# A hybrid attention and GLA layer: work beside the projections held to its place, key, GLA and merge transposes later, key tiles in other buffers

## The chip, the cores and the metric

One core of a Trainium2 chip. The metric is device time of one execution in microseconds (us); the kernel before took 2056.09 us, the median of three runs (2054.43 to 2057.13).

## The reference, cut to what matters

One layer over 256 latent tokens with 256 context tokens ahead, width 2048, all in float32. Two token mixers work side by side on one input projection.

```python
h  = rms_norm(x, g_mix) * (1 + scale) + shift         # shift, scale, gates: silu(c) @ w_mod + b_mod
qa, ka, va, qb, kb, vb, rb, lrf, lrb, gate_a, gate_b = split(h @ w_in)
o_attn = windowed_attention(rope(rms_norm(qa)), rope(rms_norm(ka)), va, ctx keys and values, sink)
o_gla  = latent_gla(qb, kb, vb, gf, gb, end states of the context)      # 4 heads, both directions
y = sigmoid(gate_a) * (o_attn @ w_attn_o) + sigmoid(gate_b) * ((rms_norm(o_gla) * silu(rb)) @ w_gla_o)
x = x + gate * (y @ w_out)
x = x + gate2 * conv_ffn(modulate(rms_norm(x)))
```

## The kernel before, in words

**Projections.** Every projection multiplies by weights streamed from memory in pieces of 256 x 512 float32 (512 KB). `wsplit` (L156) loads a piece (`raw`, 7 buffers), ScalarE copies it to `whi` (L61), and VectorE subtracts to `wlo` (L62), 3 buffers each. For each left side a product is then three matmuls: high and low part of the left side by `whi`, high part by `wlo`. `proj_nat` (L165) leaves tokens on the partitions, one bank of 512 columns for each left side (four with the context: 24 products a piece; two without: 12 products, and 8 pieces a block of columns); `proj_T` (L185) leaves features there. Four accumulation banks are shared by all; `evac` copies a finished bank.

**Order of the stages.** Five groups of the first projections while the modulation is computed; a low-rank gate; four GLA heads, each beside one projection (`with_gla`, L639, with the generator `gla_A`, L491); the keys of the attention (KA, `ka_evac`, L705) and its values (VA); queries and attention; the GLA's output gate (RB, `rb_evac`, L821); four rounds of merge, each of GA, `w_attn_o`, GB, `w_gla_o` (`mg_evac`, L855); `w_out`; the feed-forward part.

**Work beside.** Ahead of each piece `tick` (L133) is called. It takes the deferred functions from the front of the list `later` whose count has run out (transposes mostly, put there by `defer`), advances the generator in `beside` by its rate, and takes steps from `bg_steps` at `bg_rate`. These steps (`mod_latent`, L242) compute the later modulation: they load a 512 KB piece of `w_mod` into the same 7 `raw` buffers and multiply and add it on VectorE (`macc`, L266); after eight pieces a column sum is taken and a small product `pcl` (L276) deferred. The rate is 0.3 in the GLA heads, 1.6 in KA and VA, 0.52 from RB on.

**What sets the order.** A scheduler orders each engine's instructions; `wsplit` has a raised priority. Nothing but data ties a small product issued in a tick to the large products around it. All loads keep their order on SyncE's queue.

**The places of the change.** In a GLA head, `gla_A` yields after each of eight levels (products `pa`, L534) and, after the tiles kf and kg are made by scans, exponentials and two multiplications (L579 to L593), once before their products (L599), which `gla_o` (L605) needs. `norm_rope` (L682) takes a bank to a normalised, rotated tile: copy y (tag fc), squares sq (tag fc), sum, reciprocal root, products; the tile ends in sq. The tag fc has 6 buffers, fa 4; fa holds the GLA's and the attention's tiles. `to_T` (L813) transposes a finished tile for RB and the merge (`pto`), `turn` in `ka_evac` the key tiles (`ptk`).

Of the kernel before, what the change touches and what calls it, by code (L numbers as in the profile page):

```python
# [16 lines left out]
P = 128  # L17
# [13 lines left out]
def layer_kernel(ctx, tc, A, out):  # L31
# [28 lines left out]
    def split(hi, lo, src):  # L60
        S.activation(hi, src, AF.Copy)  # L61
        V.tensor_tensor(lo, src, hi.bitcast(F32), op=ALU.subtract)  # L62

# [69 lines left out]
    def tick():  # L133

        for e in later:
            e[0] -= 1
        while later and later[0][0] < 0:
            later.pop(0)[1]()
# [6 lines left out]
        while bg_rate[1] >= 1.0 and bg_steps:  # L145
            bg_rate[1] -= 1.0
            bg_steps.pop(0)()

# [16 lines left out]
    def proj_nat(w, r0, c0, kts, lhs, evac):  # L165

        banks = [acc.tile([P, 512], F32, name="acc", tag="acc") for _ in lhs]
        for k0 in kts[::2]:
# [3 lines left out]
            for i, l in enumerate(lhs):  # L172
                for k in range(nk):
                    kt = k0 + k
                    ahi, alo = l(kt)
                    PE.matmul(banks[i], ahi, hi[:, k, :], start=(kt == kts[0]), stop=False)  # L176
                    PE.matmul(banks[i], alo, hi[:, k, :], start=False, stop=False)  # L177
            for i, l in enumerate(lhs):
                for k in range(nk):
                    kt = k0 + k  # L180
                    PE.matmul(banks[i], l(kt)[0], lo[:, k, :], start=False, stop=(kt == kts[-1]))  # L181
# [3 lines left out]
    def proj_T(w, c0, kts, rhs, evac):  # L185
# [4 lines left out]
        for k0 in kts[::2]:  # L190
# [3 lines left out]
            for part in range(2):  # L194
                for f in range(4):
                    for k in range(nk):
                        kt = k0 + k
                        w_ = (lo if part else hi)[:, k, f * P:(f + 1) * P]
                        for i, r in enumerate(rhs):
# [3 lines left out]
                            PE.matmul(o, w_, ahi, start=(kt == kts[0] and b == 0 and part == 0),  # L203
                                      stop=(kt == kts[-1] and part == 1), skip_group_check=True)
                            if part == 0:
                                PE.matmul(o, w_, alo, start=False, stop=False, skip_group_check=True)  # L206
# [35 lines left out]
    def mod_latent(parts):  # L242
# [11 lines left out]
        def step(i):  # L254
# [13 lines left out]
            if k0 == KT - 2:  # L268
# [5 lines left out]
                def out():  # L274
                    pc = bank("pcl", (32, 16))
                    PE.matmul(pc, sel[:, 0:32], rs, start=True, stop=True)  # L276
# [11 lines left out]
    def rows_from_cols(name, col):  # L288

        pt = bank("pt_" + name, (KT, P), side=True)  # L290
        PE.transpose(pt, col, ident)
# [199 lines left out]
    def gla_A(h, kb, qb, res):  # L491
# [7 lines left out]
        for d in range(2):  # L499
            g_ = W2("fc", "gc", [P, 2, T])  # L500
            for dt in range(2):
                f = 2 * h + dt
                pz = bank("pz", side=True)
                PE.matmul(pz, wg[:, f * P:(f + 1) * P], lr[:, d, :], start=True, stop=True)
# [14 lines left out]
        for t in range(2):  # L519
            for dt in range(2):  # L520
                PE.matmul(pa[:, t, :], k_[:, dt, t * P:(t + 1) * P], q_[:, dt, t * P:(t + 1) * P],
# [7 lines left out]
        def products(lv, q2, k2):  # L529
            pa = bank("pa", (P, 2, P), side=True)  # L530
            for t in range(2):
                tq = t if lv < 7 else 1 - t
                for dt in range(2):
                    PE.matmul(pa[:, t, :], k2[:, dt, t * P:(t + 1) * P],  # L534
# [59 lines left out]
        yield  # L594
        pa = bank("pa", (P, 2, T), side=True)
        for t in range(2):
            for i, (kk, qq) in enumerate(((kf, q2), (kg, q3))):
                for dt in range(2):
                    PE.matmul(pa[:, t, :], kk[:, dt, t * P:(t + 1) * P], qq[:, dt, :],  # L599
# [5 lines left out]
    def gla_o(h, a, vh, vl):  # L605
# [3 lines left out]
        for t in range(2):  # L609
            po = bank("po", side=True)  # L610
            n = 0
            for s in range(4):
# [6 lines left out]
                for x_, y_ in ((ah, vh), (ah, vl), (al, vh)):  # L619
                    PE.matmul(po, x_, y_[:, s, :], start=(n == 0), stop=(n == 11))  # L620
# [18 lines left out]
    def with_gla(h, kb, block):  # L639
        res = []  # L640
        beside[:] = [gla_A(h, kb, qbt, res), 1.5, 0.0]
# [40 lines left out]
    def norm_rope(b, r, t):  # L682

        y = W2("fc", "y", [P, 4, P])
# [20 lines left out]
    def ka_evac(i, b):  # L705
        z = norm_rope(b, rk if i < 2 else None, i % 2)

        def turn():
            pt = bank("ptk", (P, 4, P))
            for h in range(4):  # L710
                PE.transpose(pt[:, h, :], z[:, h, :], ident)
            split(kTh[:, :, i * P:(i + 1) * P], kTl[:, :, i * P:(i + 1) * P], pt)

        defer(1 + i // 2, turn)
# [7 lines left out]
    def qa_block(g):  # L722
        qT = M("qT", [P, 2, 4, T], F32R)

        def evac(t, b):
            z = norm_rope(b, rq, t)
# [279 lines left out]
```

## Time and profile before

| | |
|---|---|
| median of three runs | 2056.09 us |
| profiled execution | 2061.47 us, span 2059.7 us, mean granted clock 0.989 |
| GLA heads | 232 to 485 us |
| KA and VA | 485 to 580 us |
| queries, attention, GA | 580 to 800 us |
| RB | 800 to 853 us |
| merge | 853 to 1205 us |
| w_out, feed-forward part | 1205 to 2060 us |

The lines in the next sections are from one profiled execution, in us. PE is TensorE, DVE VectorE, ACT ScalarE, SP SyncE, POOL GpSimd. A row of the timeline has start, length, engine, line and operation, what it writes and reads, a count of equal neighbours, and in brackets how long the engine waited ahead of it and for what. A row of the windows has the stretch, its length, the busy time of each engine with its instructions, the granted clock, the share of the DMA engines and their GB/s.

### The profile page before, as it was taken

Reading aid. Unit: us, or ns where it says so; the run is one execution under the profiler, and the core shown is the slowest. Engines: PE = TensorE matmul, PEld = TensorE weight load, DVE = VectorE, ACT = ScalarE, POOL = GpSimd, SP = SyncE. Lnnn points to the kernel's source line nnn. Section 1 sums busy time; section 2 is a strip of 40 time slices with the busy share of each in tenths; the row PEclk is TensorE's granted clock in tenths of the full one; section 3 lists DMA queues with packets and bytes.
Section 4 is the critical chain, followed back from the end, with each engine's and each line's share of the span. In section 5 each row is a group of like instructions: output and inputs, shape, how many; then the busy total and the mean of one; then the engine's idle time right before and its main releaser. Section 6 shows DMA issues by size and latency. Waiting matters only on the chain.

```text
span 2059.7 us, 30028 instructions
## 1 busy us (share of the span) xinstructions
PE 1998.4 (97%) x11792; PEld 1727.0 (84%) x11792; DVE 1399.2 (68%) x2149; ACT 932.7 (45%) x1306; POOL 38.9 (2%) x62
## 2 busy tenths in 40 slices
PE   6999999999999999999999999899999999999998
PEld 4778888888787777788788888899999889999987
DVE  4657577887758888777776455877787455556654
ACT  4323464552345665444344444544445334445532
POOL 0001000001000000000000000000000000000000
PEclk8999999999999999999999999899999999999999
DMA  9977322346553466788886766576776666666563
GB/s 346 360 261 217 95 82 83 92 134 203 162 153 113 135 194 198 254 274 273 275 267 218 230 211 205 177 252 226 235 260 208 201 192 191 182 182 183 184 214 112
DMA packets 214350, 413.71 MB, mean 201 GB/s; under 512 B 12548, under 2 KB 21092, under 8 KB 213184
## 3 DMA queue, kind: packets, MB, share of 16 engines
q1 hardware_dynamic: 212320, 406.89, 62.0%
q0 software_dynamic: 1360, 4.74, 0.8%
q8 instruction: 92, 1.51, 0.3%
q14 instruction: 50, 0.41, 0.1%
q10 hardware_dynamic: 528, 0.17, 0.0%
HBM read 409.63 MB, written 2.11 MB: 200 GB/s over the span
## 4 chain that ended last, share of the span: by engine, by line
PE 78%; DVE 9%; DMA 8%; ACT 2%; issue 2%; DVEq 0%; POOL 0%; ACTq 0%; SPq 0%
PE acc L203 20%; PE acc L176 13%; PE acc L177 13%; PE acc L181 13%; PE acc L206 10%; DMA raw<-in_w_mod 8%; DVE wlo L62 3%; DVE macc L266 3%; PE pm L227 1%; PE pa L534 1%; PE po L620 1%; ACT whi L61 1%; PE pa L599 1%; PE ptp L776 1%; PE poa L782 0%
## 5 line engine op out<-in xcount | busy, mean ns | idle before, releaser
L61 ACT ACTIVATE whi<-raw 128x1024 fp32r<-128x1024 f32 x568 | 601.0, 1060 | 833.9 <-PE acc L177 512.4
L62 DVE TENSOR_TENSOR wlo<-raw,whi 128x1024 fp32r<-128x1024 f32 x568 | 693.9, 1226 | 359.6 <-ACT whi L61 327.0
L203 PE MATMUL acc<-h2h,whi 128*128 128x256 f32 x1408 | 347.4, 284 | 1.5 <-ACT h2h L377 1.5
L206 PE MATMUL acc<-h2l,whi 128*128 128x256 f32 x1408 | 346.9, 284 | 0.0
L266 DVE SCALAR_TENSOR_TENSOR macc<-raw,ccol,macc 128x512 f32<-128x512 f32 x240 | 180.3, 751 | 137.3 <-DMA raw<-in_w_mod 133.9
L203 PEld LDWEIGHTS acc<-h2h,whi 128*128 128x128 f32 x1408 | 271.5, 193 | 2.0 <-ACT h2h L377 1.8
L206 PEld LDWEIGHTS acc<-h2l,whi 128*128 128x128 f32 x1408 | 271.4, 193 | 0.2
L203 PE MATMUL acc<-h2h,wlo 128*128 128x256 f32 x1408 | 198.5, 284 | 1.7 <-DVE wlo L62 1.7
L203 PEld LDWEIGHTS acc<-h2h,wlo 128*128 128x128 f32 x1408 | 182.4, 193 | 1.9 <-DVE wlo L62 1.9
L176 PE MATMUL acc<-whi,h00hi 128*128 128x512 f32 x352 | 141.0, 400 | 0.9 <-DVE kb L394 0.6
L176 PE MATMUL acc<-whi,h01hi 128*128 128x512 f32 x352 | 139.8, 397 | 0.0
L177 PE MATMUL acc<-whi,h00lo 128*128 128x512 f32 x352 | 139.7, 397 | 0.0
L177 PE MATMUL acc<-whi,h01lo 128*128 128x512 f32 x352 | 137.8, 391 | 0.0
L176 PE MATMUL acc<-whi,ah 128*128 128x512 f32 x352 | 137.1, 389 | 0.0
L177 PE MATMUL acc<-whi,al 128*128 128x512 f32 x352 | 137.0, 389 | 0.0
L181 PE MATMUL acc<-wlo,h00hi 128*128 128x512 f32 x352 | 98.2, 394 | 0.0
L181 PE MATMUL acc<-wlo,h01hi 128*128 128x512 f32 x352 | 96.9, 393 | 0.5 <-DVE wlo L62 0.5
L181 PE MATMUL acc<-wlo,ah 128*128 128x512 f32 x352 | 94.1, 389 | 0.0
L176 PEld LDWEIGHTS acc<-whi,h00hi 128*128 128x128 f32 x352 | 66.7, 190 | 14.7 <-ACT h00hi L377 0.7
L181 PEld LDWEIGHTS acc<-wlo,h00hi 128*128 128x128 f32 x352 | 66.1, 189 | 13.9 <-DVE wlo L62 0.3
L181 PEld LDWEIGHTS acc<-wlo,ah 128*128 128x128 f32 x352 | 66.1, 188 | 13.8
L176 PEld LDWEIGHTS acc<-whi,ah 128*128 128x128 f32 x352 | 66.1, 188 | 13.7
(369 smaller groups left out, 3267.7 us busy)
## 6 DMA issues: line engine op xcount, KB each, us to landing
raw<-in_w_in SPq DMA_DIRECT2D x208, 512.0 KB, 4.4
raw<-in_w_up SPq DMA_DIRECT2D x176, 512.0 KB, 3.9
raw<-in_w_mod SPq DMA_DIRECT2D x128, 512.0 KB, 4.2
raw<-in_w_down SPq DMA_DIRECT2D x88, 512.0 KB, 4.3
mraw<-in_w_mod SPq DMA_DIRECT2D x32, 1024.0 KB, 12.0
raw<-in_w_attn_o SPq DMA_DIRECT2D x32, 512.0 KB, 4.7
raw<-in_w_gla_o SPq DMA_DIRECT2D x32, 512.0 KB, 5.1
raw<-in_w_out SPq DMA_DIRECT2D x32, 512.0 KB, 4.1
```

The lines of the kernel that those rows point to most:

```text
L61: S.activation(hi, src, AF.Copy)
L62: V.tensor_tensor(lo, src, hi.bitcast(F32), op=ALU.subtract)
L176: PE.matmul(banks[i], ahi, hi[:, k, :], start=(kt == kts[0]), stop=False)
L177: PE.matmul(banks[i], alo, hi[:, k, :], start=False, stop=False)
L181: PE.matmul(banks[i], l(kt)[0], lo[:, k, :], start=False, stop=(kt == kts[-1]))
L203: PE.matmul(o, w_, ahi, start=(kt == kts[0] and b == 0 and part == 0), stop=(kt == kts[-1] and part == 1), skip_group_check=True)
L206: PE.matmul(o, w_, alo, start=False, stop=False, skip_group_check=True)
L227: PE.matmul(a[0][q:q + 32, :], cS[:, kt, :], raw[:, k, :], start=(kt < 4), stop=(kt >= 12))
L266: V.scalar_tensor_tensor(a[0], raw[:, k, :], ccol[:, kt:kt + 1], a[0], op0=ALU.mult, op1=ALU.add)
L534: PE.matmul(pa[:, t, :], k2[:, dt, t * P:(t + 1) * P], q2[:, dt, tq * P:(tq + 1) * P], start=(dt == 0), stop=(dt == 1))
L599: PE.matmul(pa[:, t, :], kk[:, dt, t * P:(t + 1) * P], qq[:, dt, :], start=(i == 0 and dt == 0), stop=(i == 1 and dt == 1))
L620: PE.matmul(po, x_, y_[:, s, :], start=(n == 0), stop=(n == 11))
```

## The change

- A large product records itself (`mm`). Within a tick, `pin` holds the last large product ahead of it, and small products and transposes made there (`mm_b`, `turn_b`: pz, pa, po, pcl, ptk, ptq, ptp, pS, poa, pto, ptx1) get an ordering dependency on it: they may not be put ahead of it on TensorE.
- `tick` runs every deferred function that is due, no longer only those at the front of the list.
- `gla_A` yields once more ahead of the kf and kg products, and its rate is 1.65 for 1.5.
- Deferral of key transposes: 2 + i ticks for 1 + i // 2; of the gated GLA tiles and the merged tiles: 3 + t for 1 + t.
- The copy y of a key tile is taken from tag fa; that of a query tile stays in fc.

```diff
+    last, pin = [None], [None]
+    def mm(*a, **k):
+        last[0] = PE.matmul(*a, **k).ins
+    def after(i):
+        if pin[0] is not None:
+            tc.add_manual_dep(i.ins, pin[0].name, mybir.DependencyInfo(
+                mybir.DependencyClass.NoSync, mybir.DependencyReason.DATA), reason="place among the products")
+        return i
+    def mm_b(*a, **k):
+        return after(PE.matmul(*a, **k))
+    def turn_b(*a):
+        return after(PE.transpose(*a))
...
     def tick():
+        pin[0] = last[0]
         for e in later:
             e[0] -= 1
-        while later and later[0][0] < 0:
-            later.pop(0)[1]()
+        due = [e for e in later if e[0] < 0]
+        later[:] = [e for e in later if e[0] >= 0]
+        for e in due:
+            e[1]()
...
+        pin[0] = None
...
-                    PE.matmul(banks[i], ahi, hi[:, k, :], start=(kt == kts[0]), stop=False)
+                    mm(banks[i], ahi, hi[:, k, :], start=(kt == kts[0]), stop=False)
...
         V.tensor_tensor(kg, kg, kc, op=ALU.mult)
         yield
+        yield
...
-        beside[:] = [gla_A(h, kb, qbt, res), 1.5, 0.0]
+        beside[:] = [gla_A(h, kb, qbt, res), 1.65, 0.0]
...
-    def norm_rope(b, r, t):
-        y = W2("fc", "y", [P, 4, P])
+    def norm_rope(b, r, t, tag):
+        y = W2(tag, "y", [P, 4, P])
...
-        z = norm_rope(b, rk if i < 2 else None, i % 2)
+        z = norm_rope(b, rk if i < 2 else None, i % 2, "fa")
...
-                PE.transpose(pt[:, h, :], z[:, h, :], ident)
+                turn_b(pt[:, h, :], z[:, h, :], ident)
...
-        defer(1 + i // 2, turn)
+        defer(2 + i, turn)
...
-            defer(1 + t, lambda: to_T(s_, gh, gl, j, t))
+            defer(3 + t, lambda: to_T(s_, gh, gl, j, t))
...
-            defer(1 + t, lambda: to_T(a2[t], mh, ml, j, t))
+            defer(3 + t, lambda: to_T(a2[t], mh, ml, j, t))
```

No instruction comes or goes: each engine has as many as before, and SyncE's order is the same. In attention, `w_out` and the feed-forward part the order of TensorE is the same too. In the rows below, line numbers of the change are 23 or 24 higher; every large product shows L68, every `turn_b` L81.

VectorE at the end of the GLA head beside VB's second block (q: `q2` and `q3` of L574; ats: the split product of the last two levels; the scans that make kf and kg show as SCALAR_TENSOR_TENSOR), before:

```order
L578 TENSOR_TENSOR q_3254<-q_3254,qb 128x512
L62 TENSOR_TENSOR ats<-at,ats 128x256
L266 SCALAR_TENSOR_TENSOR macc<-raw,ccol,macc 128x512 x2
L270 STREAM_TRANSPOSE mtr<-macc 128x512
L62 TENSOR_TENSOR wlo<-raw,whi 128x1024
L62 TENSOR_TENSOR ats<-pa,ats 128x256
L584 SCALAR_TENSOR_TENSOR kf<-ones,gc 128x256
```

The same place now, on to the multiplication of kf and kg:

```order
L601 TENSOR_TENSOR q_3224<-q_3224,qb 128x512
L62 TENSOR_TENSOR ats<-at,ats 128x256
L62 TENSOR_TENSOR ats<-pa,ats 128x256
L607 SCALAR_TENSOR_TENSOR kf<-ones,gc 128x256
...
L611 TENSOR_SCALAR tot<-kf 128x2
L289 SCALAR_TENSOR_TENSOR macc<-raw,ccol,macc 128x512 x2
L62 TENSOR_TENSOR wlo<-raw,whi 128x1024
L615 TENSOR_TENSOR kf<-kf,kb_451 128x512
L616 TENSOR_TENSOR kg<-kg,kb_451 128x512
```

The scans moved ahead of the maccs, the transpose and the `wlo`; the maccs and a `wlo` now stand between the scans and kf. On TensorE the products of kf and kg stood behind 22 products of that block's last piece in this head, 20 in the next and 24 in the last; now behind 11, 9 and 10.

VectorE behind the KA block (s: the sum of squares; y and sq as in `norm_rope`), before, from the first finished rstd to the first finished key tile:

```order
L318 TENSOR_TENSOR rstd<-rstd,newt 128x4
L316 TENSOR_TENSOR newt<-newt,msq 128x4 x2
L691 TENSOR_TENSOR y<-y,rstd 128x512
L317 TENSOR_SCALAR newt<-newt 128x4 x2
L697 TENSOR_TENSOR sq<-y,att 128x4x64 x2
L318 TENSOR_TENSOR rstd<-rstd,newt 128x4 x2
L699 TENSOR_TENSOR y<-y,att 128x512
L691 TENSOR_TENSOR y<-y,rstd 128x512
L700 TENSOR_TENSOR sq<-sq,y 128x512
```

The same stretch now:

```order
L341 TENSOR_TENSOR rstd<-rstd,newt 128x4 x2
L62 TENSOR_TENSOR wlo<-raw,whi 128x1024
L715 TENSOR_TENSOR y<-y,rstd 128x512 x2
L721 TENSOR_TENSOR sq<-y,att 128x4x64 x3
L723 TENSOR_TENSOR y<-y,att 128x512
L721 TENSOR_TENSOR sq<-y,att 128x4x64
L724 TENSOR_TENSOR sq<-sq,y 128x512
```

A `wlo` and both half products of the second tile moved ahead of the first finished tile, and further up the sum of squares of the fourth tile, which stood behind all of these rows, stands with the three others.

TensorE behind the KA block, whose last products read h10 and h11 and the VA block's first ones h00 (hi and lo parts), before:

```order
L181 MATMUL acc<-wlo,h00hi 128x512 x4
L181 MATMUL acc<-wlo,h10hi 128x512 x2
L176 MATMUL acc<-whi,h00hi 128x512
L711 MATMUL ptk<-ident,sq 128x128 x4
L177 MATMUL acc<-whi,h00lo 128x512
L176 MATMUL acc<-whi,h10hi 128x512
```

And now:

```order
L68 MATMUL acc<-wlo,h00hi 128x512 x4
L68 MATMUL acc<-wlo,h10hi 128x512 x4
L81 MATMUL ptk<-ident,sq 128x128 x4
L68 MATMUL acc<-whi,h00hi 128x512
L68 MATMUL acc<-whi,h00lo 128x512
```

The first key transposes stood inside VA's second and third piece, behind 37 products of VA; now they stand behind two whole pieces, 48 products, since all four banks of VA go on at once. In RB and the merge the transposes `pto` of a tile stand two pieces of 12 products later than before, and those of the two tiles of a block, where they stood together (the merge's first), one piece apart.

44 lines of the change are left out of this document (22 added, 22 removed).

## Prediction

> **What bounds the kernel now.** The page first: the span, the engines' shares, the chain that ended last.
>
> ```profile
> span 2059.7 us, 30028 instructions
> PE 1998.4 (97%) x11792; PEld 1727.0 (84%) x11792; DVE 1399.2 (68%) x2149; ACT 932.7 (45%) x1306; POOL 38.9 (2%) x62
> PE 78%; DVE 9%; DMA 8%; ACT 2%; issue 2%; DVEq 0%; POOL 0%; ACTq 0%; SPq 0%
> ```
>
> TensorE is busy 97% of the span, so a change that removes no product can win at most its waits; and for 17% of the span the chain runs over VectorE and the DMA, so in some stages TensorE is not what sets the end. Where it waits (line, releaser, total us, times, longest):
>
> ```profile
> PE ptk L711 <- DVE sq L700: 5.0, 1, 5.0
> PE pa L599 <- DVE kf L592: 4.9, 4, 2.1
> PE pto L816 <- DVE sr L826: 3.9, 1, 3.9
> PE pa L534 <- DVE q L554: 3.4, 4, 1.5
> PE pto L816 <- DVE m L857: 3.2, 2, 2.3
> PE acc L181 <- DVE wlo L62: 1.2, 3, 0.5
> ```
>
> These are the waits that the edits can reach, 21.6 us. Some cost more than their length, because the granted clock is low behind them (windows; the number ahead of the last two is the clock):
>
> ```profile
> 541.85:544.00 2.15, 2.15 (x7) 1.91 (x8) 2.15 (x5) 1.53 (x3) 0.00 (x0) 0.50 0.00 0
> 544.00:546.00 2.00, 2.00 (x6) 1.56 (x5) 0.88 (x2) 1.04 (x2) 0.00 (x0) 0.50 0.00 0
> 859.80:862.00 2.20, 2.18 (x8) 1.88 (x9) 2.20 (x4) 0.60 (x1) 0.00 (x0) 0.59 0.78 237
> 862.00:864.00 2.00, 2.00 (x7) 1.56 (x6) 1.76 (x4) 0.10 (x1) 0.00 (x0) 0.60 0.74 209
> 1028.00:1030.00 2.00, 2.00 (x6) 1.61 (x5) 1.93 (x8) 0.00 (x0) 0.00 (x0) 0.50 0.87 300
> 1030.00:1032.00 2.00, 2.00 (x8) 1.56 (x8) 1.26 (x3) 1.06 (x1) 0.00 (x0) 0.78 0.83 283
> 346.40:350.00 3.60, 3.59 (x17) 3.19 (x18) 1.89 (x3) 1.53 (x4) 0.00 (x0) 1.00 0.00 0
> ```
>
> Lost to the clock, window by one minus the clock: 1.1 + 1.0 = 2.1 us behind the ptk wait, 0.9 + 0.8 = 1.7 us behind the wait for sr, 1.0 + 0.4 = 1.4 us behind those for m. Behind the longest kf wait (2.09 us) nothing is lost. With these 5.2 us the reachable sum is 26.8 us, 1.3% of the time. The work is to see how much of it goes.
>
> **Keys: 0.** Timeline rows of VectorE and TensorE (start, length, what, count, wait):
>
> ```profile
> 535.04 1.27 DVE L689 TENSOR_REDUCE s<-sq 128x4 f32<-128x512 f32 x2
> 539.08 0.76 DVE L697 TENSOR_TENSOR sq<-y,att 128x256 f32<-128x256 f32 x2
> 541.11 0.69 DVE L700 TENSOR_TENSOR sq<-sq,y 128x512 f32<-128x512 f32 x1
> 541.85 1.12 PE L711 MATMUL ptk<-ident,sq 128*128 128x128 f32 x4 [5.01 <-DVE sq L700]
> 854.64 0.39 PE L177 MATMUL acc<-whi,ol 128*128 128x512 f32 x1
> 854.87 1.07 PE L181 MATMUL acc<-wlo,oh 128*128 128x512 f32 x4
> ```
>
> The last two rows give the step from product to product in a stream, 0.23 us (2.72 us for the 12 of a block with two left sides). The key transposes had their place at 536.84, 37 products behind the last of the key block, and waited for the first finished tile. Now they stand 48 products behind it: 11 x 0.227 = 2.5 us later. But the tile comes later too. With y in buffers of their own the fourth bank is copied at once, and the order on VectorE puts more ahead of the first tile: one more reduction (0.6), one more `wlo` (1.2) and both half products of the second tile (0.7): 2.5 us, so 544.3 instead of 541.8. Place and tile move alike; the stall and its slow clock stay, and I count 0. Ends: -7.1 (5.0 + 2.1) if the tile is as early as before and the place far enough behind it, +1.5 if a `wlo` in that queue waits itself. The three later tiles then stand 24 products (5.4 us) apart, against about 2.5 us of VectorE for each.
>
> **RB and merge: -4.** The stall of 3.9 + 1.7 us goes: the gated tile is made from 859.00 on, and its transposes, whose place was 855.94, move behind two more blocks (24 products, 5.4 us), to 861.4. The m transposes likewise stand one block apart and two blocks later. What is late next is the weights:
>
> ```profile
> 851.35 2.36 DVE L62 TENSOR_TENSOR wlo<-raw,whi 128x1024 fp32r<-128x1024 f32 x2
> 859.00 1.28 DVE L826 TENSOR_TENSOR sr<-sr,og 128x512 f32<-128x512 f32 x2
> 863.71 1.09 PE L181 MATMUL acc<-wlo,oh 128*128 128x512 f32 x4
> 863.90 1.06 ACT L61 ACTIVATE whi<-raw 128x1024 fp32r<-128x1024 f32 x1 [2.71 <-PE acc L177]
> 865.00 1.23 DVE L62 TENSOR_TENSOR wlo<-raw,whi 128x1024 fp32r<-128x1024 f32 x1 [1.20 <-ACT whi L61]
> 976.56 1.22 DVE L62 TENSOR_TENSOR wlo<-raw,whi 128x1024 fp32r<-128x1024 f32 x1
> 977.83 1.21 PE L181 MATMUL acc<-wlo,h00hi 128*128 128x512 f32 x4
> 1082.25 1.22 DVE L62 TENSOR_TENSOR wlo<-raw,whi 128x1024 fp32r<-128x1024 f32 x1
> 1085.33 0.84 PE L181 MATMUL acc<-wlo,h01hi 128*128 128x512 f32 x3
> ```
>
> The slack of a block is the start of its wlo products less the end of its `wlo`. At 863.71, just behind the stall, it is 863.71 - 853.71 = 10.0 us. At 977.83 it is 977.83 - 977.78 = 0.05, at 1085.33 1.86. So the lead that the stall gave the weights is used up within 114 us, and then TensorE goes at the weights' pace. The chain of waits of this stage names the pace:
>
> ```profile
> 868.30 4.04 DMA raw<-in_w_mod
> 872.43 0.76 DVE macc L266
> ...
> 904.05 3.91 DMA raw<-in_w_mod
> ```
>
> A w_mod load of some 4 us, two maccs, and only then the next load, since it wants the buffer that they free: six rounds from 868.30 to 904.05, 5.96 us each. TensorE asks for 0.52 of one in each block (`bg_rate`, L806), one in 2.72 / 0.52 = 5.23 us. While VectorE stands in a macc for its load, the `wlo` behind it in its queue stand too. Take away 5.6 us of stall, and TensorE comes to the end of the lead 40 to 50 us earlier and waits there instead. What is kept until the m waits (1023 on) is only what the stall had cost the weights themselves: ScalarE stood 2.7 us for TensorE ahead of the `whi` at 863.90, and VectorE 1.2 us for that `whi`; I take 2.1, between the two. Then the m waits (3.2 + 1.4) go, and the smallest slack left until the w_mod loads end is the 1.86 at 1085: another 1.9. Sum -4.0. Ends: -1.9 if nothing of the first is kept, and the whole of 3.9 + 1.7 + 3.2 + 1.4 + 1.2 = -11.4 if the weights could go faster once TensorE frees them earlier.
>
> **GLA: 0.** Head 1 (and, at 403.60, one row of head 2), VectorE and TensorE:
>
> ```profile
> 336.36 0.42 DVE L62 TENSOR_TENSOR ats<-at,ats 128x256 fp32r<-128x256 f32 x1
> 337.89 1.54 DVE L266 SCALAR_TENSOR_TENSOR macc<-raw,ccol,macc 128x512 f32<-128x512 f32 x2 [1.11 <-DMA raw<-in_w_mod]
> 341.54 0.68 DVE L584 TENSOR_TENSOR_SCAN kf<-ones,gc 128x256 f32<-128x256 f32 x1
> 345.57 0.69 DVE L592 TENSOR_TENSOR kf<-kf,kb 128x512 f32<-128x512 f32 x1
> 403.60 1.22 DVE L62 TENSOR_TENSOR wlo<-raw,whi 128x1024 fp32r<-128x1024 f32 x1 [2.21 <-ACT whi L61]
> 346.41 1.10 PE L599 MATMUL pa<-q,kf 128*128 128x256 f32 x4 [2.09 <-DVE kf L592]
> ```
>
> The scans now stand right behind the two ats, at about 337.2 instead of 341.54. Between them and kf come the maccs (1.5) and a `wlo` (1.2), while a reduction (0.7) and kg (0.7) leave: kf is ready at 345.57 + 0.69 - 4.3 + 1.3 = 343.2, 3 us earlier. Its place was 344.3 and moves 11 products forward, to 341.8: a wait of 1.4 in place of 2.09, with the wait of the last level's product, also earlier, in it. Head 2 moves 11 forward (2.5 us); there the `wlo` at 403.60, for which VectorE stood still 2.2 us, no longer lies ahead of the scans: 2.2 won, +0.3. Head 3 moves 14 forward (3.2); the order takes four maccs, a reduction and kg from ahead of its kf and puts a macc, a transpose and again a `wlo` there, some 2 us won: +1.2. Head 0 stays. The first level's products of heads 2 and 3 stand three products later (0.7), so that their waits on q ((3.4 - 1.5) / 3 = 0.6 each) go: -1.2. Sum -0.4, called 0; ends -4 (half of 4.9 + 3.4) and +8.2 (the places forward by 2.5 + 2.5 + 3.2, nothing won), before any slow clock.
>
> [...]
>
> All else (attention, w_out, FFN) keeps its order, and SyncE's loads theirs. POOL has one swap, the rope table's load ahead of the mask's, outside any wait of TensorE.
>
> **The sum.** 0 - 4 + 0 = -4 us. The profiled execution took 2061.47 us (span 2059.7 and 1.8 around it), so it would take 2057.5; that execution lies 5.4 us above the median of the runs, 2056.09, which gives 2052.
>
> **Rivals.**
> 1. *The stalls go for good.* For it: the `wlo` row at 865.00 shows the weights held by TensorE. Against it: the chain of waits lies on the w_mod loads, not on TensorE, through that stage. -11.4 with the keys at 0 gives 2045; with part of the keys' 7.1 too, down to 2038.
> 2. *Slower: the GLA's earlier places.* The kf and kg products, pinned 11 to 14 products forward, wait for a VectorE that is not earlier. It decides at a gain of VectorE's of 2.7 us a head, the mean shift: with none, the waits of 2.09 and (4.9 - 2.09) / 3 = 0.9 become 4.6, 3.4 and 4.1 us, with the slow clock's 1.7 behind each: 8.2 + 5.1 - 4 = +9, 2065; with half of it won, +4 - 4 + the clock behind one = 2058 to 2061. For it: the waits there are short because TensorE had filled them with products that are now pinned. Against it: the scans do move ahead of 3 us of other work.
> 3. *It changes the order and not the time.* Readiness, not place, sets every one of these waits, and the weights take back the rest: 2056, within 1 us.
>
> **How the numbers follow.** The forecast 0.50 (own range 2048 to 2056), rival 1 0.22, rival 2 0.20, rival 3 0.08. A measurement of this kernel can tell about 0.2%, 4.1 us, from no change: below 2052.0 is faster, above 2060.2 slower. The forecast lies on the lower bound: I give 0.23 of its 0.50 to faster and 0.27 to the same. Rival 1 is faster, rival 3 the same, rival 2 slower but for 0.02. Faster 0.45, same 0.37, slower 0.18. The range takes in the forecast, rival 1 but for its deepest part, rival 3 and the near part of rival 2: 2041 to 2062.
>
> **What would show it.** Keys: a ptk wait of about 5 us at 544 and the clock 0.50 behind it; wrong if it is under 2. RB and merge: no pto wait over 0.5 us, but more waits of the products for `wlo` or `whi` between 890 and 1025 than the 1.2 us of before, 4 to 6 us in all, and w_mod loads in the chain there; wrong if the stage from 853 to the last merge block is shorter by 8 us or more. GLA: kf waits of about 1, 1.4, 1.3 and 2.1 us in the four heads; wrong if they sum to over 8. The forecast falls as a whole if stages whose order is kept change by more than 2 us.

## The result and the profile after

No change: the changed kernel took 2057.83 us in the median of twelve runs (2053.64 to 2060.99), the kernel before 2055.68 in twelve (2053.12 to 2058.92); the ratio is 1.0010 with a 95% interval of 1.0001 to 1.0019. Two more comparisons, on two chips, gave 1.0001 (0.9988 to 1.0015) and 1.0002 (0.9990 to 1.0013). The same kernel before against itself gave 1.0001 (0.9992 to 1.0011) and 1.0004 (0.9990 to 1.0018), so such a comparison leaves at least 1 us uncertain. The forecast was 2052, 4 us faster.

The page of the changed kernel, which took 2057.55 us in its profiled execution:

```profile
span 2055.8 us, 30016 instructions
PE 1997.9 (97%) x11792; PEld 1722.0 (84%) x11792; DVE 1399.4 (68%) x2149; ACT 932.4 (45%) x1306; POOL 42.4 (2%) x62
PE 51%; DMA 11%; DVE 6%; issue 1%; ACT 1%; DVEq 0%; ACTq 0%
```

And TensorE's waits there (line, releaser, total us, times, longest; the line is the helper's):

```profile
PE acc L68 <- DVE wlo L62: 5.9, 11, 1.0
...
PE pa L78 <- DVE q L577: 3.5, 4, 1.5
PE ptx L81 <- DVE x L903: 2.9, 2, 2.2
...
PE pa L78 <- DVE kf L615: 2.5, 4, 1.0
PE po L78 <- DVE v3l L62: 2.3, 1, 2.3
PE ptk L81 <- DVE sq L724: 1.8, 1, 1.8
...
PE ptx L81 <- issue: 1.1, 1, 1.1
```

Against before: the pto waits (3.9 and 3.2) are gone, the key wait fell from 5.0 to 1.8, the kf waits from 4.9 to 2.5. New are the waits for `wlo` (5.9 instead of 1.2 and 1.7), one of po for v3l, and one of ptx at 1220.53, which before did not have. The old waits were exchanged for others.

One trace of each is not enough here: the profiled execution of before (2061.47 us) lies above all twelve of its timed runs, that of the change amid its own. So marks were taken in three traces of each: the first gate product (pz), the first copies of KA's and of the first query block's banks (y), of RB's last block (sr), the first multiplication of the last merge block (m), the last low product of w_out (mh), the first of the feed-forward part, the end. Lengths in us between them:

| from one mark to the next | before, three traces | changed, three traces | mean difference |
|---|---|---|---|
| GLA heads and KA | 294.8, 294.4, 294.6 | 298.0, 298.0, 297.9 | +3.3 |
| keys, VA, first query block | 77.1, 76.5, 76.3 | 72.0, 74.4, 74.3 | -3.1 |
| attention to RB's end | 249.0, 249.3, 249.1 | 249.2, 248.9, 248.5 | -0.3 |
| merge | 345.6, 346.0, 345.6 | 341.2, 339.3, 342.5 | -4.7 |
| w_out | 91.5, 91.5, 91.5 | 92.8, 93.3, 95.6 | +2.4 |
| to the feed-forward part | 11.0, 12.2, 10.5 | 11.8, 10.6, 11.1 | -0.1 |
| feed-forward part | 758.3, 755.8, 756.8 | 757.8, 755.1, 757.3 | -0.2 |

The edits' own rows sum to -2.1 us (3.3 - 3.1 - 4.7 + 2.4); the timed runs say between 0 and +2. Two stretches win and two lose; the experiments ask why.

The traced executions are not average ones. Those of before lie 5.8, 2.3 and 0.7 us above the medians of the timed runs beside them, those of the change 0.3 and 5.2 below and 1.9 above. So the traced spans of the change are 3.0 us shorter in the mean (0.4 of it ahead of the first mark), where the medians are 1.1 us longer. The table can be trusted for a stretch in which all three traces of one kernel lie on one side of all three of the other, and not for the sum.

### The profile page after: what moved, and what is told of

Read it like the earlier page. It is cut to its first block, busy times and chain, and to the rows that moved or that the text cites. A ratio compares the mean times of both kernels' runs of the same rounds, so it can differ in the third digit from the quotient of the medians.

```text
span 2055.8 us, 30016 instructions
## 1 busy us (share of the span) xinstructions
PE 1997.9 (97%) x11792; PEld 1722.0 (84%) x11792; DVE 1399.4 (68%) x2149; ACT 932.4 (45%) x1306; POOL 42.4 (2%) x62
## 4 chain that ended last, share of the span: by engine, by line
PE 51%; DMA 11%; DVE 6%; issue 1%; ACT 1%; DVEq 0%; ACTq 0%
PE acc L68 48%; DMA raw<-in_w_mod 11%; DVE macc L289 3%; DVE wlo L62 2%; PE poa L78 1%; PE pS L78 1%; PE ptp L81 1%; ACT whi L61 0%; PE ptq L81 0%; PE pto L81 0%; DVE u L948 0%; DMA raw<-in_w_up 0%; DVE macc L287 0%; PE ptx L81 0%; DVE u L950 0%
## 5 line engine op out<-in xcount | busy, mean ns | idle before, releaser
L68 PE MATMUL acc<-h2h,whi 128*128 128x256 f32 x1408 | 347.1, 284 | 1.5 <-ACT h2h L400 1.5
L68 PE MATMUL acc<-h2l,whi 128*128 128x256 f32 x1408 | 346.6, 284 | 0.0
L68 PEld LDWEIGHTS acc<-h2h,whi 128*128 128x128 f32 x1408 | 271.2, 193 | 2.0 <-ACT h2h L400 1.8
L68 PEld LDWEIGHTS acc<-h2l,whi 128*128 128x128 f32 x1408 | 271.2, 193 | 0.2
L68 PE MATMUL acc<-h2h,wlo 128*128 128x256 f32 x1408 | 198.0, 283 | 1.5 <-DVE wlo L62 1.5
L68 PEld LDWEIGHTS acc<-h2h,wlo 128*128 128x128 f32 x1408 | 181.5, 192 | 2.3 <-DVE wlo L62 2.3
L68 PE MATMUL acc<-whi,h00hi 128*128 128x512 f32 x352 | 140.5, 399 | 1.1 <-DVE val L62 0.5
L68 PE MATMUL acc<-whi,h01hi 128*128 128x512 f32 x352 | 139.9, 398 | 0.0
L68 PE MATMUL acc<-whi,h00lo 128*128 128x512 f32 x352 | 138.3, 393 | 0.0
L68 PE MATMUL acc<-whi,h01lo 128*128 128x512 f32 x352 | 138.0, 392 | 0.0
L68 PE MATMUL acc<-whi,ah 128*128 128x512 f32 x352 | 137.0, 389 | 0.0
L68 PE MATMUL acc<-whi,al 128*128 128x512 f32 x352 | 137.0, 389 | 0.0
L68 PE MATMUL acc<-wlo,h01hi 128*128 128x512 f32 x352 | 97.3, 394 | 1.1 <-DVE wlo L62 1.0
L68 PE MATMUL acc<-wlo,h00hi 128*128 128x512 f32 x352 | 97.7, 393 | 0.3 <-DVE wlo L62 0.3
L68 PE MATMUL acc<-wlo,ah 128*128 128x512 f32 x352 | 94.1, 389 | 0.0
L68 PEld LDWEIGHTS acc<-whi,h00hi 128*128 128x128 f32 x352 | 66.4, 189 | 15.0 <-DVE val L62 1.0
L68 PEld LDWEIGHTS acc<-wlo,h01hi 128*128 128x128 f32 x352 | 65.4, 188 | 15.9 <-DVE wlo L62 2.7
L68 PEld LDWEIGHTS acc<-wlo,h00hi 128*128 128x128 f32 x352 | 65.8, 188 | 14.1 <-DVE wlo L62 0.7
L68 PEld LDWEIGHTS acc<-wlo,ah 128*128 128x128 f32 x352 | 66.1, 188 | 13.7
```

The costliest lines, as they stand in the source:

```text
L68: last[0] = PE.matmul(*a, **k).ins
```

## The experiments

Each kernel gave a trace with these marks and 10 to 12 timed runs (5 for the two that leave work out). Both kernels were run again, twice each, to see the scatter; `undo_` kernels are the change with one part put back, `_only` ones the kernel before with one part.

**before_2, after_2, after_3, before_3: the scatter.**

> The kernel before, once more, for a second trace. The first trace of before (2061.5 us) lies above all twelve timed runs of before (2053.1 to 2058.9), that of the change (2057.6) amid its own. Theory A, the stalls and the slow clock of before are the same in every execution and the 5.4 us above the median were lost elsewhere: this trace again shows the waits of 5.0 (ptk), 3.9 (sr) and 3.2 us (m), and is shorter in stages that the change does not touch. Theory B, these waits differ from run to run: they are shorter here by some 4 us in all, most of it between 800 and 1030 us.

> The changed kernel, once more, for a second trace. Against the trace of before its first one was 5.4 us ahead at the RB and merge stages, 3.9 at the end, as forecast, although the timed runs have it 2 us slower. Theory A: the same stalls as in its first trace within 1 us, and the RB and merge stages again 4 us shorter than in before. Theory B: the stages from 800 to 1205 us differ from its first trace by 3 us or more.

> The changed kernel a third time. By the marks in the traces its stages sum to 2 us less than before's (GLA and KA +3.4, up to the first query block -3.3, RB and merge -3.7, w_out +1.9), by the timed runs it is 1 to 2 us slower. If the marks are right: within 2 us of before, on the faster side. If the timed runs are: 1 to 2 us slower, and a stage in this trace, changed or not, shows it.

> The kernel before a third time, on the same chip as the three others: its difference from the runs of before that go with them is the noise of such a comparison, which I take for 1 us. The marks as in its other traces: 294.4 to 294.8 us for GLA and KA, 342 to 346 for RB's end to the last merge block, 91.5 for w_out.

before_2 took 2057.26 us in the median and before_3 2057.64, against 2056.56 and 2057.56 for before's own runs beside them; after_2 2057.69 and after_3 2058.39. Theory B is right in that the waits differ: before's second trace had

```profile
PE pto L816 <- DVE m L857: 3.8, 2, 3.0
PE acc L181 <- DVE wlo L62: 3.3, 5, 0.9
PE pto L816 <- DVE sr L826: 2.6, 1, 2.6
```

and a key wait of 3.83 instead of 5.01. It is not right in the size: the waits named are 1.9 us shorter in all, not 4, the merge is as long as in the first trace, and 2.5 us were won in the feed-forward part, which the change does not touch, as theory A had it. For after_2 theory A holds: its waits for po, ptk, ptx and `wlo` in the merge are within 1 us of those in the change's first trace, and its merge is again over 4 us shorter than before's. The waits that hang on transfers were not the same in two executions (5.01 and 3.83 us at the keys, 3.9 and 2.6 at sr); a forecast from one trace carries that. Between the marks most stretches of before agree within 1 us, so the differences of over 2 us in the table stand. Two stretches of the change vary more: the merge from 339.3 to 342.5 us, w_out from 92.8 to 95.6. after_3 has the worst of both, and its stretches against the means of before give +3.2 - 2.4 - 0.6 - 3.2 + 4.1 = +1.1 us, where the table's means give -2.4 for these five. The stage that loses most in it is w_out, which the forecast had left at nothing.

**undo_gla and gla_h3: where the GLA part loses 3.3 us.**

```diff
-        yield
-        yield
+        yield
...
-        beside[:] = [gla_A(h, kb, qbt, res), 1.65, 0.0]
+        beside[:] = [gla_A(h, kb, qbt, res), 1.5, 0.0]
```

> The change with the generator of the GLA heads back at a rate of 1.5 and without the second yield. The trace of the change has the GLA heads about 1 us shorter than before. Theory of the forecast: within 1 us of the change. Rival, the earlier places with ordering dependencies cost there: 2 us faster than the change; if the rate and the yield are what makes up for the dependencies: 3 us or more slower.

It took 2056.42 us (ratio to before 0.9996, 0.9983 to 1.0009), 1.3 us less than after_2 beside it, which by itself settles nothing; but GLA and KA took 294.6 us, as before. So the loss is in the rate and the second yield, not in the ordering dependencies. In the trace of the change the kf waits had become shorter, and a wait of po was new. TensorE, then VectorE, at the end of head 3 in the change:

```profile
471.35 1.10 PE L78 MATMUL pa<-q,kf 128*128 128x256 f32 x4 [0.42 <-DVE kf L615]
...
478.08 0.71 PE L78 MATMUL po<-v3h,ats 128*128 128x512 f32 x2
481.09 0.50 PE L78 MATMUL po<-v3l,ats 128*128 128x512 f32 x1 [2.30 <-DVE v3l L62]
```

```profile
475.95 0.68 DVE L62 TENSOR_TENSOR atc<-pa,atc 128x512 fp32r<-128x512 f32 x1
476.55 2.49 DVE L289 SCALAR_TENSOR_TENSOR macc<-raw,ccol,macc 128x512 f32<-128x512 f32 x3
478.96 1.48 DVE L62 TENSOR_TENSOR wlo<-raw,whi 128x1024 fp32r<-128x1024 f32 x1
480.36 1.87 DVE L62 TENSOR_TENSOR v3l<-acc,v3h 128x512 fp32r<-128x512 f32 x3
```

The same place in before, TensorE and VectorE:

```profile
473.12 1.07 PE L181 MATMUL acc<-wlo,h11hi 128*128 128x512 f32 x4
474.97 1.10 PE L599 MATMUL pa<-q,kf 128*128 128x256 f32 x4 [0.79 <-DVE kf L592]
...
478.31 0.58 PE L620 MATMUL po<-v3h,ats 128*128 128x512 f32 x1
```

```profile
476.54 2.48 DVE L62 TENSOR_TENSOR v3l<-acc,v3h 128x512 fp32r<-128x512 f32 x4
```

In before the 16 products of kf and kg (3.5 us) stood behind the last VB product, and while they ran VectorE made v3l. In the change they run inside the block; po follows the last VB product directly, and v3l stands behind three maccs and a `wlo`. The wait of 2.3 us is the cover that went, and the clock fell behind it (windows of the change, clock ahead of the last two numbers):

```profile
480.00:483.00 3.00, 1.91 (x7) 1.53 (x8) 3.00 (x6) 0.00 (x0) 1.87 (x5) 0.88 0.84 269
483.00:485.00 2.00, 2.00 (x7) 1.51 (x6) 1.93 (x3) 0.00 (x0) 0.00 (x0) 0.50 0.67 250
485.00:487.00 2.00, 2.00 (x9) 1.64 (x8) 1.89 (x4) 1.18 (x3) 0.00 (x0) 0.83 0.76 231
```

By the granted clock these windows lose 0.4 (3.00 at 0.88), 1.0 (2.00 at 0.50) and 0.3 us (2.00 at 0.83), 1.7 together. gla_h3 puts back the cover in this one head:

```diff
-        beside[:] = [gla_A(h, kb, qbt, res), 1.65, 0.0]
+        beside[:] = [gla_A(h, kb, qbt, res), 1.65 if h < 3 else 1.5, 0.0]
...
         yield
-        yield
+        if h < 3:
+            yield
```

> The change, with rate 1.5 and one yield for the last GLA head only, so that its kf and kg products again stand between the last VB product and the output products. Theory: the GLA's loss in the change (298.0 us from the first gate product to the end of KA, 294.6 in before) is the lost cover at that place, a 2.3 us wait of po for v3l with the slow clock behind it: 294.6 to 295.5 here; and the wait for the first key tile, which is set by VectorE's w_mod chain and not by TensorE, grows by the same 2 to 3 us, so that the sum up to the first query block stays at 370 to 372.

```profile
473.19 1.10 PE L78 MATMUL pa<-q,kf 128*128 128x256 f32 x4 [1.02 <-DVE kf L615]
...
476.53 0.81 PE L68 MATMUL acc<-wlo,h11hi 128*128 128x512 f32 x2
477.18 0.39 PE L78 MATMUL po<-v3h,ats 128*128 128x512 f32 x1
```

No wait of po, and 294.2 us for GLA and KA: the first half of the theory is shown. The second half fell: the key wait did not grow (2.1 us), the stretch up to the first query block stayed at 73.9, the sum is 368.1 and not 370 to 372. It took 2053.73 us, 0.9976 of before (0.9968 to 0.9985): faster by more than its interval.

**keys_only and undo_keys: the keys.** keys_only adds to before

```diff
-        z = norm_rope(b, rk if i < 2 else None, i % 2)
+        z = norm_rope(b, rk if i < 2 else None, i % 2, "fa")
...
-        defer(1 + i // 2, turn)
+        defer(2 + i, turn)
```

and undo_keys takes the same out of the change.

> The kernel before with the key edits alone: y of the keys in fa, deferral 2 + i. Forecast's step: place and tile move alike, 0 within 1.5 us, a wait of about 5 us at the first key transposes. Rival: the trace of the change had only 1.8 us there, so it may win 3 us and the slow clock's 2: 3 to 5 us faster than before.

> The change with the key edits taken back (y in fc, deferral 1 + i // 2). If the keys win 3 to 5 us: slower than the change by that, with a wait of about 5 us and the slow clock behind it. If they win nothing: within 1 us of the change.

In keys_only the first key transposes had their place 11.82 us behind the mark of KA's end, where before had 9.57, and the tile was there at 16.41 (before 14.60, 13.40, 13.22):

```profile
543.08 1.11 PE L711 MATMUL ptk<-ident,sq 128*128 128x128 f32 x4 [4.59 <-DVE sq L700]
```

That is the forecast's step: place 2.25 later, tile 2.1 later behind the first reduction (8.9 us instead of 6.8), wait unchanged, 76.95 us for the stretch. The timed runs were 0.9983 of before (0.9973 to 0.9993), a gain of 3.4 us in the mean. Its traced execution, at 2057.66, lies 3.3 above its median, and its only stretch over 2 us shorter than before's is the merge (342.3), where it has nothing of the change; keys_merge below, with the same edit, does not have the gain. undo_keys took 2055.56 (0.9993, 0.9982 to 1.0004), 2 to 3 us less than the change, and its first key transposes, which stood 14.07 us behind the mark, waited for nothing: both of its expectations missed. What the key edits are worth by themselves stays open within some 3 us; a mechanism for a gain was not found.

The stretch is some 3 us shorter in the kernels with the GLA at 1.65 (gla_h3 and both_mends in three heads), with or without the key edits (72.0 to 74.6 in eight traces, undo_keys 72.8; 75.4 to 77.7 in nine of ten with 1.5, but 74.2 in bare_before). There VectorE's backlog of w_mod work is gone earlier: the first reduction of the key squares starts 4.7 to 5.8 us behind KA's end, in kernels with 1.5 throughout 5.6 to 7.9. In the first trace of the change the tile was then ready in time for a wait of 1.82, with a clock of 1.00 from 541 to 551; the wait was 2.72 in after_2, with 0.84 and 0.82 in the two windows of 5 us from 541, and 2.54 in after_3, and both have a stretch 2.3 to 2.4 us longer. The first trace:

```profile
544.73 0.66 PE L81 MATMUL ptk<-ident,sq 128*128 128x128 f32 x4 [1.82 <-DVE sq L724]
...
541.00:546.00 5.00, 3.18 (x17) 2.38 (x16) 5.00 (x10) 1.65 (x2) 0.00 (x0) 1.00 0.33 105
```

That it is earlier also in gla_h3, whose GLA is not longer, says that this is not the GLA's loss absorbed by the key wait. Why the w_mod work is further ahead was not settled.

**pins_only: the ordering dependencies alone.** The change with 1.5, one yield, and the old deferrals and buffers.

> The change without its new numbers: ordering dependencies and the list of due functions, but rate 1.5, one yield, the old deferrals and y in fc. Theory: the dependencies alone change nothing, within 1 us of before, since the trace of undo_gla shows GLA heads of the same 251.5 us. Rival: the dependencies cost and the new numbers make up for them: 3 us or more slower than before.

2058.99 us, 1.0006 of before (0.9997 to 1.0015): nothing beyond the scatter. Its trace had a wait of 1.93 us for kf in head 1 (2.09 in before's first trace) with a clock of 0.72 over the 6 us behind it, which cost 1.7 us there and makes its GLA and KA 296.4 us long; without it they would take 294.6, as before.

**merge_only, undo_merge and keys_merge: the later transposes.** merge_only adds to before, undo_merge takes out of the change:

```diff
-            defer(1 + t, lambda: to_T(s_, gh, gl, j, t))
+            defer(3 + t, lambda: to_T(s_, gh, gl, j, t))
...
-            defer(1 + t, lambda: to_T(a2[t], mh, ml, j, t))
+            defer(3 + t, lambda: to_T(a2[t], mh, ml, j, t))
```

> The change with the deferral of the gated and the merged tiles put back to 1 + t. If the weights take back what the stalls give (the theory of the forecast), the time stays within 2 us of the change, up to 4 us longer, and the waits of TensorE for the low weights in the merge fall from 5.9 us to about 1. If the later transposes themselves cost (a rival), it is 2 us faster than the change. If the stalls were a real loss, it is 8 to 11 us slower.

> The kernel before with nothing changed but the deferral of the gated and merged tiles, 3 + t for 1 + t, without ordering dependencies. In five traces so far the stage from the first product of w_attn_o to the first of w_out took 346 us with 1 + t and 340 to 343 with 3 + t, and w_out 1 to 2 us more. If this is a gain that every execution has: 3 to 4 us faster than before. If the weights take it back (theory of the forecast, in its stronger form): within 1 us of before, with more than 4 us of waits for the low weights in that stage.

> The kernel before with the key edits and the later gated and merged tiles, without ordering dependencies and with the old GLA order. If the parts add up (keys_only 3.4 us faster in the mean, merge_only 0.5): 3 to 5 us faster than before. If keys_only was an accident of its runs: 0 to 2 us faster.

undo_merge took 2059.91 us (1.0015 of before, 1.0001 to 1.0030), 2.2 more than after_2 beside it, merge_only 2056.95 (0.9997 of before, 0.9986 to 1.0009), keys_merge (merge_only with keys_only's edit) 2056.35 (0.9994, 0.9981 to 1.0006). In the merge 1 + t gave 342.3 to 346.0 us (six traces) and 3 + t 339.1 to 342.9 (ten, both_mends and last_early below among them); w_out took 91.5 with 1 + t in the last round (92.7 in both_mends alone) and 92.6 to 95.6 with 3 + t. So the later transposes win some 3.5 us in the merge in the mean, though the two groups touch at 342.3 to 342.9, and give back 1 to 4 in w_out. The waits for low weights rise in the merge (1.2, 3.3 and 2.4 us in before, 4.4, 4.7 and 5.6 in the change), but not between 890 and 1025, where the forecast had placed 4 to 6 us: there the change has 2.7, 2.0 and 4.0. Changed kernel, TensorE's waits from 853 to 1194:

```profile
PE acc L68 <- DVE wlo L62: 4.4, 7, 1.0
```

**bare_before and bare_merge: the merge without the w_mod work.** From RB on the loads of w_mod and their multiply-adds are left out, so that part of the modulation is not computed; bare_merge has the deferral 3 + t.

```diff
-            get(i)
-            get(i + 1)
+            if not bare[0]:
+                get(i)
+                get(i + 1)
...
-            for k in range(2):
+            for k in range(0 if bare[0] else 2):
...
     bg_rate[0] = 0.52
+    bare[0] = True
```

> The kernel before, leaving out the w_mod loads and their multiply-adds from RB to the end of the merge (two modulation vectors are then not computed). Theory, the w_mod supply takes back what the stalls cost: here the weights are never late, the stalls for sr and m stay as long as VectorE needs for the tiles, up to 5 us in the first merge round, with the slow clock behind them; RB's end to the end of w_out takes 431 to 434 us instead of 434 to 437.

> The same without the w_mod work, with the deferral of the gated and merged tiles at 3 + t. Theory: now nothing takes the gain back, so it is faster than bare_before by the whole of its sr and m waits and the clock behind them, and no product waits for low weights. Rival, the later transposes give little for a reason of their own (banks, ScalarE): it gains no more than the 2 us that the full kernels show between the same marks.

In both the theory that was expected is wrong: bare_before has no stall in the merge to lose, and bare_merge is not faster. The window of bare_before from 853 to 1180:

```profile
853.00:1180.00 327.00, 327.00 (x1460) 269.42 (x1459) 171.10 (x187) 139.12 (x142) 0.00 (x0) 1.00 0.64 197
```

TensorE does not stop once, with the transposes where before has them, and the merge takes 331.9 us in the one and 332.1 in the other. So the sr and m stalls were not VectorE's time for the tiles: they went with the w_mod work. In before it stands ahead of the tile in VectorE's queue, itself waiting for its load:

```profile
855.68 1.54 DVE L266 SCALAR_TENSOR_TENSOR macc<-raw,ccol,macc 128x512 f32<-128x512 f32 x2 [1.97 <-DMA raw<-in_w_mod]
...
857.89 1.18 DVE L62 TENSOR_TENSOR wlo<-raw,whi 128x1024 fp32r<-128x1024 f32 x1
859.00 1.28 DVE L826 TENSOR_TENSOR sr<-sr,og 128x512 f32<-128x512 f32 x2
```

Whether its loads or its multiplications weigh more was not separated. The work costs the merge 13.8 us in before (345.7 - 331.9) and 9.1 in the change (341.0 - 331.9). bare_before took 2044.74 us (0.9934 of before, 0.9922 to 0.9946), bare_merge 2049.28 (0.9950, 0.9938 to 0.9963): with nothing to win in the merge, bare_merge is 4.5 us slower. Of these w_out shows 2.6 (91.5 and 94.1), with one wait that bare_before did not have; 2.8 more lie in the two traces at the keys (74.2 and 77.1), where the two kernels are the same, so they are not the transposes':

```profile
PE ptx L890 <- issue: 2.4, 1, 2.4
```

**last_early and both_mends: the wait in w_out, and a version that wins.** The transposes of the last merge round fall into the first block of w_out, and a chain begins there too: the gate column is turned (pt_gate), stored as a row (dgate) and loaded again as a row for all partitions (gate), which every w_out block needs. pt_gate stands 8.3 us behind the last merge tile in before and in the change; but in the change the second tile's transposes now stand directly ahead of it, and ScalarE copies that tile (at 1205.72) ahead of the row (1206.22), so that the store is issued 0.3 us later. POOL in before, in the change, and in last_early:

```profile
1211.85 0.52 POOL L295 DMA_DIRECT2D dgate<-row  x1 [407.16 <-ACT row L293]
1214.43 0.55 POOL L297 DMA_DIRECT2D gate<-dgate  x1 [2.06 <-PE acc L181]
```

```profile
1206.76 0.52 POOL L318 DMA_DIRECT2D dgate<-row  x1 [402.85 <-ACT row L316]
1210.91 0.55 POOL L320 DMA_DIRECT2D gate<-dgate  x1 [3.64 <-PE acc L68]
```

```profile
1205.74 0.52 POOL L318 DMA_DIRECT2D dgate<-row  x1 [403.62 <-ACT row L316]
1208.24 0.55 POOL L320 DMA_DIRECT2D gate<-dgate  x1 [1.98 <-PE acc L68]
```

Store to load is 2.6 us in before and 4.2 in the change. The releaser named, a product, is only what came last by the profile; the small store itself lands 2.0 us after its issue in before and 3.5 in the change. Counted from the mark of the last merge block the load is issued 15.3 to 15.6 us later in eight traces with 1 + t in the last round (15.5 in last_early), and 17.5 to 17.8 in all nine with 3 + t. In the three traces of before the row landed 0.1 to 0.9 us ahead of its first use; in the change the first use waited, and TensorE behind it:

```profile
1218.00 0.69 DVE L902 TENSOR_TENSOR yo<-acc,gate 128x512 f32<-128x512 f32 x1 [2.53 <-DMA gate<-dgate]
...
1220.53 0.63 PE L81 MATMUL ptx<-ident,x 128*128 128x128 f32 x4 [1.07 <-issue]
```

This wait was 1.1, 1.6 and 2.4 us in the three traces of the change. after_3, with the longest, lost 4.1 us in w_out (95.6 - 91.5), 1.7 beyond the wait, as much as the slow clock cost behind the po wait; that it was slow clock here too is the author's estimate.

```diff
-            defer(3 + t, lambda: to_T(a2[t], mh, ml, j, t))
+            defer((3 if j < 3 else 1) + t, lambda: to_T(a2[t], mh, ml, j, t))
```

> The change with the last merge round's tiles deferred as before (1 + t in the last round, 3 + t in the others). Theory: the 1.0 to 2.4 us wait at the first transposes of w_out comes from those two tiles, whose later transposes push the gate row's small store and with it its broadcast load 2.2 us back: here that load is issued 15.3 to 15.6 us behind the last merge tile again (17.5 to 17.8 in the change), no such wait, 91.5 us from the last merge block to the end of w_out instead of 92.5 to 93.5; 1 to 2 us faster than the change.

> As last_early, and the last GLA head at rate 1.5 with one yield (as gla_h3, 4.3 us faster than before in the mean). Theory: both losses of the change gone, 294.2 us for GLA and KA, 91.5 for w_out: 5 to 6 us faster than before, 4 to 6 faster than the change. If gla_h3's gain was an accident of its runs: within 2 us of the change.

last_early: w_out 91.5 us, no such wait, 2055.32 us, 3.1 less than after_3 beside it (0.9989 of before, 0.9977 to 1.0001). both_mends, this and gla_h3's edit together: 2050.11 us, 0.9966 of before (0.9954 to 0.9977), the fastest kernel of the study that computes everything, 7 us ahead of before, where 5 to 6 were expected. GLA and KA took 294.1 us. In w_out a wait of 0.95 us was left in its trace, the slowest of its twelve timed runs (92.7 us), with the load issued at 16.0: the small store took 2.4 us there to land, for a reason that no run shows. Against the means of before its trace wins 4.2 us at the keys and 4.1 in the merge; why the keys win stays open, as above.

## Why the prediction was wrong

Two terms that the sum had at nothing failed: the GLA and, in "all else", w_out. A third, the keys, won where 0 was forecast.

*The bound, and the reachable 26.8 us.* The list of waits was right; its sizes were those of one execution. Three traces of before have 5.0, 3.8 and 3.7 us at the keys, and 3.9, 2.6 and 3.0 at sr.

*Keys: 0.* Right as a step: the place moved 2.25 us (forecast 2.5), the tile 2.1 (2.5), and keys_only has the same wait as before. In the changed kernel the stretch was nonetheless 3.1 us shorter. The w_mod work ahead of it had cleared earlier: the waits were 1.8, 2.7 and 2.5 us where before has 5.0, 3.8 and 3.7, with a clock of 1.00 behind the first and 0.84 and 0.82 (541 to 546 and 546 to 551) behind the second, where the first trace of before has 0.50 from 539.35 to 546.18. By the forecast's own sign (a wait under 2 us) it was wrong in the first trace and not in the others. The forecast took the start of the chain, 535.04, as given by KA; it was given by VectorE's backlog.

*RB and merge: -4.* The size was right (-4.7 between the marks) and so was the direction of the reason: the w_mod work still costs 9.1 of 13.8 us, of which 4.4 to 5.6 are waits for low weights; the rest stands in no wait. Its picture of two opponents, stalls by VectorE's tiles and a supply by w_mod, was not: in bare_before, without the w_mod work, both are gone. And the step's end was set at the last merge block. The sentence "All else (attention, w_out, FFN) keeps its order" is **the step that failed** for this term: TensorE's order in w_out is unchanged but for the very transposes that were deferred into it, and what stands behind them there, the gate's store and load, had 0.1 to 0.9 us to spare. w_out lost 2.4 us, over the 2 us by which the forecast said it would fall as a whole, and last_early gives them back. Why a store issued 0.3 us later takes 1.6 to 2 us longer to land (3.5 to 3.9 us against 1.9 in the mean), no run shows.

*GLA: 0.* **This step failed** by 3.3 us. The kf waits fell to 2.5 us in all, where the forecast had 5.8, and the q waits stayed at 3.5, where -1.2 was counted; neither decided. What was left out is the question asked elsewhere, what is late next: the products of kf and kg were the cover for v3l, and when they moved 14 products forward in head 3, po had none. 2.3 us and 1.7 of slow clock; gla_h3 took them away, and the stretch is as short as before's. The rows named give -2.4 (kf) + 2.3 (po) + 1.7 (clock) = +1.6 us; the other 1.7 of the 3.3 stand in no wait: with waits and slow clock taken off, the stretch is 286.5 us in before, 288.0 in the change and still 287.6 in gla_h3, with the same products, and why stays open. It is rival 2's sign and place, not its mechanism: that one had kf late, and kf was early.

*The sum.* -4 was forecast; between the marks it is +3.3 - 3.1 - 4.7 + 2.4 = -2.1, of which 5.7 us are two losses that were not in the working and 3.1 a gain that was not. The timed runs show 0 to +2 instead of -2. The traced executions account for the difference in the sum, those of before lying above their medians and one of the change far below its own; in which stretch it would vanish stays open (the loss in w_out alone varies from 1.3 to 4.1 us between traces). A gain of 0.2% lies outside all three intervals.

*The slow clock.* The forecast counted it from the rows of one trace: 5.2 us behind the waits at the keys, sr and m, and 1.7 behind each long wait of rival 2. In the later rows the po wait of 2.30 us alone was followed by a granted clock of 0.50 (483 to 485), one of 2.91 in undo_merge by 0.67 (546 to 551), the 1.82 us at the keys by 1.00 (541 to 551). Behind the po wait the slow clock cost 1.7 us, as rival 2 had it for each: almost the wait's length again.

## What to carry to other kernels

A piece of work that is moved leaves its place empty: ask what it covered there, and what stands behind the place that it moves to, in the next stage too if it crosses into it. A stall in one engine's order and a shortage of weights were one and the same queue here (in bare_before TensorE was busy for all 327.00 us of the merge's window); taking the suspected work out (two kernels, one with each order) says so at once, and says how much can be won at all. Where a wait hangs on transfers, read it in several executions before it is priced, and see where these lie among the timed runs before their spans are compared.

## What the runs showed of the hardware

A wait of 2.30 us in the change was followed by a granted clock of 0.50 over 2 us, and one of 2.91 in undo_merge by 0.67 over 5; waits of 1.82 in the change and 2.09 in before were followed by 1.00 (over 5 and 3.6 us), and one of 1.93 in pins_only by 0.72 over 6. In these five rows the length of the wait does not order the clocks: behind 1.93 us the clock was lower than behind 2.09. Of the waits that the forecast priced in before, the clock was 0.50 for 6.83 us at the keys (from 539.35, within the wait), for 3.41 at sr (from 860.20) and for 3.41 at m (from 1027.45); in the change it was 0.50 for 3.41 us behind the po wait (from 482.27). Windows of that length around the wait of 2.09 us in before and that of 2.30 in the change (TensorE's busy time stands first behind the length, the clock ahead of the last two numbers):

```profile
341.38:344.79 3.41, 2.93 (x13) 2.08 (x12) 3.30 (x10) 0.68 (x2) 0.00 (x0) 1.00 0.81 264
344.79:348.21 3.42, 1.80 (x9) 1.63 (x10) 2.58 (x5) 3.14 (x6) 0.00 (x0) 1.00 0.03 11
348.21:351.62 3.41, 3.41 (x17) 2.90 (x16) 1.70 (x3) 1.09 (x2) 0.00 (x0) 1.00 0.00 0
```

```profile
478.85:482.27 3.42, 1.18 (x5) 1.00 (x6) 3.42 (x6) 0.62 (x2) 3.02 (x6) 1.00 0.84 282
482.27:485.68 3.41, 3.41 (x10) 2.62 (x9) 3.30 (x5) 0.47 (x1) 0.00 (x0) 0.50 0.69 224
485.68:489.09 3.41, 3.41 (x16) 2.80 (x16) 1.67 (x3) 1.76 (x6) 0.00 (x0) 1.00 0.83 253
```

TensorE is idle for 1.62 us in the second window of before, and the clock is 1.00 in the next; it is idle for 2.24 in the first window of the change, and the next is at 0.50, which costs 1.7 us. What decides between the two was not shown.

A store of 8 KB from POOL landed in 2.0 us in before, 1.8 in before_2 and 1.9 in last_early, with the old order of the last round, and in 3.5 us in the change, 3.9 in after_3 and 3.9 in merge_only, with the new one; in the change it was issued 0.3 us later behind the last merge tile than in before. both_mends, with the old order, had 2.4.
